# A recurrence's affine step, bonus and gate moved to features on the partitions, and GpSimd's arithmetic moved to VectorE, in a four-layer network

## The chip, the cores and the metric

The kernel runs on one core of one Trainium2 chip. The metric is the device time of one execution in microseconds, given as the median of several runs. The change touches the first two of four layers.

## What is computed

256 tokens of width 1024 pass two layers of a first block and two layers of a second one. The change lies in the first block, whose layer mixes three branches: attention over selected keys, a short convolution, and a recurrence with heads of 64. After the recurrence come, per token and head, a normalisation, an affine step, a bonus and a gate, and then the gated sum of the branches:

```python
    mean = jnp.mean(y, axis=-1, keepdims=True)
    var = jnp.mean(jnp.square(y - mean), axis=-1, keepdims=True)
    yn = ((y - mean) * lax.rsqrt(var + RW_GN_EPS) * ln_w.astype(f32).reshape(RW_HEADS, RW_HEAD_DIM)
          + ln_b.astype(f32).reshape(RW_HEADS, RW_HEAD_DIM))
    bonus = jnp.sum(r * kf * r_k.astype(f32), axis=-1, keepdims=True) * v
    out = (yn + bonus) * g.reshape(hs)
...
        up = jnp.einsum('bsgc,gcd->bsgd', branches, w_branch[l])
        gates = jax.nn.sigmoid(gate_pre + b_gate[l]).reshape(bsz, seq, N_BRANCH, D_MODEL)
        mixed = jnp.sum(gates * up, axis=2)
        h = h + mixed @ w_out[l]
```

## The kernel before, in words

Every weight matrix streams from HBM once. A panel lands in one of two `raw` buffers (SP queue); ACT makes its rounded high part `whi` (L184) and DVE the rest `wlo` (L185), three buffers each; PE multiplies in three terms: L206, L207 and L208, each 128x128 weights against 256 columns. These matmuls of the weights are most of PE's work. They write to PSUM pool `mm`, which has three banks (L125 names the pool); a bank comes free when ACT or DVE has read it.

A layer of the first block is `mix`. Three Python generators run in it as streams, `rwkv`, `attend` and `bulk`; each yields the cost that its author gave a step, times a factor of the table TUNE, and `interleave` always continues the stream that is behind. The order in which the streams emit, with a scheduler's reordering at build, is the order on each engine, and an engine takes its instructions strictly in that order.

- `rwkv`: `rw_prepare` (gate g at L784, bonus sums at L845), `rw_scores`, then `rw_solve` beside `rw_tokens`, then `rw_chain`. `rw_solve` inverts 32 small triangular matrices by 31 steps on DVE, one multiplication (L905) and one sum (L906) each, which grow to 512 columns; all read the buffer `lb`. After it come copies (L910), transposes (L917, L919), and 64 small matmuls twice (L926, L931). `rw_tokens` turns keys and values to tokens (L875, L879 on PE; copies L876, L880, L882 on ACT), and ends in `rw_rows`, which loads the affine rows by two DMAs and calls GpSimd four times per half (L1000 to L1003). `rw_chain` walks four chunks of 64 tokens (L946 to L979), and after every second one calls `rw_finish` (normalisation, with the affine step at L1019 and L1020).
- `attend`: queries flipped (L393, L672), key duplicates `kd` (L675), `kT` (L679), scores (L445), masking (L451), exponentials (L454), probabilities flipped and applied (L486, L488, L496, L498).
- `bulk`: gates of branch 1 into the four halves of two `gate` buffers (called `m`), each a matmul of 48 (`feature_pair`), two tanh on ACT (L1028) and, in `branch`, a product on DVE (L1035); the gates `th` of branch 2, again two buffers; branch 0; and at the end branch 2. Branches 0 and 2 are added into `m` by L1038 on DVE and L1039 on GpSimd.

Big temporary tiles come from one pool, `sl`, by `slot`: 21 buffers that are handed out in turn, so that a new tile takes the buffer of the tile that was given up longest ago, and its first writer waits for that tile's last reader:

```python
        v = (self.sx if extra else self.sl).tile([128, 1024], dt, tag="s4", name=name)[:, :n]
```

The tiles `m`, `th`, `lb`, `vt`, `lnwb`, `lng`, `gt`, `qT` and the split operands `op` all come from it.

Of the kernel before, what the change touches and what calls it, by code (L numbers as in the profile page):

```python
# [9 lines left out]
F32 = mybir.dt.float32  # L10
F32R = mybir.dt.float32r
I32 = mybir.dt.int32
AF = mybir.ActivationFunctionType
ALU = mybir.AluOpType
# [3 lines left out]
S = 256  # L18
# [482 lines left out]
class Block1:  # L501
# [6 lines left out]

    def rope_tables(self):
# [38 lines left out]
    def vectors(self, l):  # L548
# [6 lines left out]
                   ("k_a", one(w["rw_k_a"][l]), 4), ("r_k", w["rw_r_k"][l].rearrange("(a b) d -> a (b d)", b=2), 4)],  # L555
# [10 lines left out]
        vec = k.sp.tile([128, 204], F32, tag="vec", name="vec", bufs=2)  # L566
# [17 lines left out]
        out["ffn"] = vec[:, 70:202]  # L584
# [168 lines left out]
    def rw_prepare(self, l):  # L753
# [27 lines left out]
        self.gt = k.slot(2, 512, name="gtok")  # L781
        for t in range(2):
            ps = k.bank(k.rk, 512)
            nc.tensor.matmul(ps, lhsT=lo[:, 1, 128 * t:128 * t + 128], rhs=gup, start=True, stop=True)  # L784
            nc.scalar.copy(self.gt[:, t], ps)
# [55 lines left out]
        self.bonus = k.sp.tile([128, 2, 8], F32, tag="bonus", name="bonus", bufs=1)  # L841
        ps = k.bank(k.rk, 2, 8)
        for t in range(2):
            for b in range(4):
                nc.tensor.matmul(ps[:, t], lhsT=kx[:, b, 128 * t:128 * t + 128], rhs=k.c["sel"][:, 8 * b:8 * b + 8], start=b == 0, stop=b == 3)  # L845
        nc.vector.tensor_copy(self.bonus, ps)
        self.ar, self.bk = ar, bk

# [18 lines left out]
    def rw_tokens(self):  # L867
# [3 lines left out]
        vt = k.slot(2, 512, name="vt")  # L871
        for c in range(4):
# [8 lines left out]
            if c % 2:  # L881
                nc.scalar.copy(vt[:, c // 2], ps.rearrange("p a b -> p (a b)"))  # L882
            yield 1.5
        self.bkt, self.uv, self.vt = bkt, uv, vt
        self.rw_rows()
# [50 lines left out]
    def rw_chain(self):  # L936
# [3 lines left out]
        for c in range(4):  # L940
# [39 lines left out]
            yield 8.0  # L980
            if c % 2:
                self.rw_finish(c // 2)
                yield 8.0
        yc = k.operand(2)
        for j in range(2):
            k.split(k.flip_pair([self.yc[:, 0], self.yc[:, 1]], j), *yc[j])
        self.yo = yc
        yield 3.0

    def rw_rows(self):  # L990

        k, nc = self.k, self.k.nc
        lw = k.slot(2, 512, name="lnwb")
        nc.scalar.dma_start(out=lw[:, 0], in_=self.w["rw_ln_w"][self.l].partition_broadcast(128))
        nc.scalar.dma_start(out=lw[:, 1], in_=self.w["rw_ln_b"][self.l].partition_broadcast(128))
        self.lg = k.slot(2, 512, name="lng")
        for t in range(2):
# [484 lines left out]
```

## Time and profile before

| | us |
|---|---|
| median of 3 runs (lowest, highest) | 1742.14 (1742.01, 1744.76) |
| the profiled execution | 1742.93 |
| its span in the trace | 1740.9 |
| PE busy / DVE busy / ACT busy / GpSimd busy | 1700.2 / 1250.7 / 957.2 / 72.4 |

The profiled execution lies 0.8 us over the median, and 2.0 us of it lie outside the span. Times in the trace count from the span's start. The first layer's mixing runs up to about 349 us; the second layer of the first block repeats it some 515 us later, in the same order. Instruction lines (L905) are those of the kernel before; where a line of the changed kernel is meant, the text says so.

### The profile page before, as it was taken

The numbers are of one execution on the slowest core, as the hardware profiler recorded it, in microseconds if no ns is written. First come the engines' busy times: TensorE is split into PE (matmuls) and PEld (weight loads), VectorE is DVE, ScalarE is ACT, GpSimd is POOL, SyncE is SP. The second block draws the span as 40 slices with busy tenths as digits, with TensorE's granted clock in tenths as the row PEclk, the third lists the DMA queues.
The fourth block names the chain that finished last, engine by engine and source line by source line (L and its number), as shares of the span: only waits on it lengthen the run. The fifth ranks groups of instructions, "written<-read, shape, count | busy, mean of one in ns | idle before, by whom it ended". The sixth has DMA issues, their size and how long they took to land.

```text
span 1740.9 us, 30007 instructions
## 1 busy us (share of the span) xinstructions
PE 1700.2 (98%) x12016; PEld 1539.7 (88%) x12016; DVE 1250.7 (72%) x2464; ACT 957.2 (55%) x1688; POOL 72.4 (4%) x81
## 2 busy tenths in 40 slices
PE   8999899999999999899999999999999999999998
PEld 8988789899989988799899987788899887888997
DVE  6699947789957689757789857576666675666666
ACT  6554633556646544633555556666564566665643
POOL 2000201101000000201000000000000000000000
PEclk9999989999999999899999999999999999999999
DMA  7534323565556444314555565344445554444454
GB/s 229 171 111 128 115 74 101 178 192 186 181 179 209 127 137 129 98 62 146 169 189 177 186 211 170 129 157 142 157 147 172 191 172 144 146 149 158 155 171 134
DMA packets 217371, 268.89 MB, mean 154 GB/s; under 512 B 6570, under 2 KB 170716, under 8 KB 217232
## 3 DMA queue, kind: packets, MB, share of 16 engines
q1 hardware_dynamic: 213520, 262.81, 46.7%
q10 hardware_dynamic: 2944, 3.94, 0.8%
q8 instruction: 94, 1.54, 0.4%
q14 instruction: 45, 0.37, 0.1%
q0 software_dynamic: 768, 0.23, 0.1%
HBM read 265.91 MB, written 1.05 MB: 153 GB/s over the span
## 4 chain that ended last, share of the span: by engine, by line
PE 81%; DVE 11%; DMA 4%; ACT 3%; issue 2%; POOL 0%; ACTq 0%; SPq 0%; POOLq 0%; DVEq 0%
PE ps L206 15%; PE ps L207 15%; PE ps L208 15%; PE ps L246 8%; PE ps L244 8%; PE ps L245 8%; DVE wlo L185 4%; PE ps L445 2%; PE ps L393 2%; DMA raw<-in_ffn_down_dram 1%; DMA raw<-in_w_in_dram 1%; ACT whi L184 1%; PE ps L486 1%; DVE pr L905 1%; PE ps L949 1%
## 5 line engine op out<-in xcount | busy, mean ns | idle before, releaser
L185 DVE TENSOR_TENSOR wlo<-raw,whi 128x1024 fp32r<-128x1024 f32 (+2 forms) x504 | 615.4, 1224 | 302.2 <-ACT whi L184 289.1
L184 ACT ACTIVATE whi<-raw 128x1024 fp32r<-128x1024 f32 (+2 forms) x504 | 525.6, 1046 | 555.9 <-PE ps L207 292.8
L206 PE MATMUL ps<-op,whi 128*128 128x256 f32 x2464 | 710.6, 288 | 0.1
L207 PE MATMUL ps<-op,whi 128*128 128x256 f32 x2464 | 703.3, 285 | 1.2 <-DVE op L199 1.0
L208 PE MATMUL ps<-op,wlo 128*128 128x256 f32 x2464 | 702.2, 285 | 1.3 <-DVE wlo L185 1.2
L206 PEld LDWEIGHTS ps<-op,whi 128*128 128x128 f32 x2464 | 474.8, 193 | 11.2 <-issue 8.5
L207 PEld LDWEIGHTS ps<-op,whi 128*128 128x128 f32 x2464 | 475.2, 193 | 6.6 <-issue 4.3
L208 PEld LDWEIGHTS ps<-op,wlo 128*128 128x128 f32 x2464 | 474.9, 193 | 3.8 <-DVE wlo L185 1.8
L244 PE MATMUL ps<-whi,op 128*128 128x512 f32 (+2 forms) x784 | 306.2, 391 | 0.8 <-ACT qtok L1200 0.8
L245 PE MATMUL ps<-wlo,op 128*128 128x512 f32 (+2 forms) x784 | 302.2, 386 | 2.5 <-DVE wlo L185 2.5
L246 PE MATMUL ps<-whi,op 128*128 128x512 f32 (+2 forms) x784 | 303.2, 387 | 1.3 <-DVE op L199 1.3
L246 PEld LDWEIGHTS ps<-whi,op 128*128 128x128 f32 x784 | 148.5, 189 | 30.0 <-DVE op L199 2.2
L245 PEld LDWEIGHTS ps<-wlo,op 128*128 128x128 f32 x784 | 148.8, 190 | 29.4 <-DVE wlo L185 3.8
L244 PEld LDWEIGHTS ps<-whi,op 128*128 128x128 f32 x784 | 148.6, 190 | 29.4 <-issue 2.0
L454 ACT ACTIVATE e<-e,m 128x128 f32<-128x128 f32 (+1 forms) x160 | 70.9, 446 | 16.2 <-DVE m L451 15.8
L451 DVE CUSTOM_DVE_ANT_0 e<-ps,consts 128x128 f32<-128x128 f32 (+1 forms) x128 | 39.1, 351 | 15.5 <-PE ps L445 13.2
L199 DVE TENSOR_TENSOR op<-xt,op 128x512 fp32r<-128x512 f32 x48 | 32.2, 687 | 19.0 <-ACT op L198 18.8
L445 PE MATMUL ps<-qT 64*128 64x256 f32 (+1 forms) x256 | 35.8, 351 | 1.0 <-DVE m L451 0.8
L488 ACT COPY pt<-ps 128x384 f32<-128x384 f32 x64 | 28.8, 480 | 12.9 <-PE ps L486 7.6
L709 DVE SCALAR_TENSOR_TENSOR glu<-ps,vec,glu 128x254 f32<-128x254 f32 x72 | 34.4, 478 | 1.4
L1039 POOL TENSOR_TENSOR gate<-gate,up 128x512 f32<-128x512 f32 x16 | 26.0, 1627 | 212.3 <-DVE up L1038 169.6
L708 DVE SCALAR_TENSOR_TENSOR glu<-ps,vec,glu 128x255 f32<-128x255 f32 x72 | 34.3, 476 | 0.2
(337 smaller groups left out, 1562.7 us busy)
## 6 DMA issues: line engine op xcount, KB each, us to landing
raw<-in_w_in_dram SPq DMA_DIRECT2D x130, 1024.0 KB, 5.2
raw<-in_ffn_up_dram SPq DMA_DIRECT2D x44, 1024.0 KB, 5.1
raw<-in_ffn_down_dram SPq DMA_DIRECT2D x20, 1024.0 KB, 5.1
raw<-in_w_out_dram SPq DMA_DIRECT2D x16, 1024.0 KB, 5.2
raw<-in_w_branch_dram SPq DMA_DIRECT2D x24, 512.0 KB, 3.4
raw<-in_w_proj_a_dram SPq DMA_DIRECT2D x8, 1024.0 KB, 5.2
raw<-in_w_proj_b_dram SPq DMA_DIRECT2D x8, 1024.0 KB, 5.2
raw<-in_w_in_dram SPq DMA_DIRECT2D x8, 768.0 KB, 4.4
```

The lines of the kernel that those rows point to most:

```text
L184: nc.scalar.activation(out=hi, in_=v, func=AF.Copy)
L185: nc.vector.tensor_tensor(out=lo, in0=v, in1=hi.bitcast(F32), op=ALU.subtract)
L206: self.nc.tensor.matmul(ps, lhsT=hi[:, k], rhs=xh, start=k == 0, stop=False)
L207: self.nc.tensor.matmul(ps, lhsT=hi[:, k], rhs=xl, start=False, stop=False)
L208: self.nc.tensor.matmul(ps, lhsT=lo[:, k], rhs=xh, start=False, stop=k == nk - 1)
L244: self.nc.tensor.matmul(ps[t][:, :n], lhsT=xh, rhs=hi, start=kk == first, stop=False)
L245: self.nc.tensor.matmul(ps[t][:, :n], lhsT=xh, rhs=lo, start=False, stop=False)
L246: self.nc.tensor.matmul(ps[t][:, :n], lhsT=xl, rhs=hi, start=False, stop=kk == last)
L393: self.nc.tensor.transpose(ps[:, a, 128 * t:128 * t + 128], src[t][:, 128 * k:128 * k + 128], self.ident)
L445: nc.tensor.matmul(ps[b][:, a:a + n], lhsT=qt[r, 128 * t:128 * t + 128], rhs=kt[r, 0:n], start=True, stop=True)
L451: nc.vector.tensor_tensor_reduce(out=e[:, a:a + n], in0=ps[b][:, a:a + n], in1=mask[:, a:a + n], scale=1.0, scalar=3e38, op0=ALU.add, op1= ...
L454: nc.scalar.activation(out=e[:, a:a + n], in_=e[:, a:a + n], func=AF.Exp, scale=-1.0, bias=m[:, t:t + 1], accum_out=z[:, 2 * b + t:2 * b + ...
```

## The change

- The gate g is computed with features on the partitions (four 128x256 matmuls, not two of 128x512); ACT also writes `gl`, g times the affine weight, in four scaled copies. The affine weight and bias come as eight more rows of the small vectors that `vectors` loads and turns, by two short DMAs more.
- The bonus sums over a head (eight matmuls with 8 columns, L845, and a copy, L846) go. `rw_bonus`, called after the chain's first chunk, multiplies by a constant `same` (ones on two 64x64 diagonal blocks) in four 128x256 matmuls, which also spreads the sum; DVE multiplies by v (two operations from PSUM), adds the bias and multiplies by g (four).
- `rw_rows` goes, with its two DMAs and eight GpSimd operations, and so do the copies `vt` (L882) and L1019, L1020. At the end of the chain DVE multiplies the flipped result by `gl` and adds g times the rest, and then the result is split.
- `branch` adds with DVE (L1041 of the changed kernel).
- With `vt`, `lnwb` and `lng` gone and `gl` new, the pool `sl` hands out two tiles fewer per layer, in another order.

```diff
@@ -505,6 +505,11 @@
         self.sd = [k.cp.tile([128, 4, 128], F32, name=f"sd{i}") for i in range(2)]
         for s in self.sd:
             k.nc.gpsimd.memset(s, 0.0)
+
+        self.same = k.cp.tile([128, 128], F32, name="same")
+        k.nc.gpsimd.memset(self.same, 0.0)
+        for i in range(2):
+            k.nc.gpsimd.memset(self.same[64 * i:64 * i + 64, 64 * i:64 * i + 64], 1.0)
 
     def rope_tables(self):
 
@@ -552,7 +557,8 @@
         two = lambda v: v.rearrange("j (r p) -> (j r) p", p=128)
         groups = [[("b_gate", one(w["b_gate"][l]), 24), ("sc", two(w["sc_conv"][l]), 12), ("mu", one(w["rw_mu"][l]), 14),
                    ("w0", one(w["rw_w0"][l]), 4), ("a0", one(w["rw_a0"][l]), 4), ("k_k", one(w["rw_k_k"][l]), 4),
-                   ("k_a", one(w["rw_k_a"][l]), 4), ("r_k", w["rw_r_k"][l].rearrange("(a b) d -> a (b d)", b=2), 4)],
+                   ("k_a", one(w["rw_k_a"][l]), 4), ("r_k", w["rw_r_k"][l].rearrange("(a b) d -> a (b d)", b=2), 4),
+                   ("ln_w", one(w["rw_ln_w"][l]), 4), ("ln_b", one(w["rw_ln_b"][l]), 4)],
                   [("ffn0", two(w["ffn_conv"][l])[0:66], 66)], [("ffn1", two(w["ffn_conv"][l])[66:132], 66)]]
         out, loads = {}, []
         for g in groups:
...
@@ -778,11 +784,14 @@
             yield 3.0
         for dst, _, _ in two:
             nc.vector.tensor_scalar(out=flat(dst), in0=flat(dst), scalar1=0.5, scalar2=0.5, op0=ALU.mult, op1=ALU.add)
-        self.gt = k.slot(2, 512, name="gtok")
-        for t in range(2):
-            ps = k.bank(k.rk, 512)
-            nc.tensor.matmul(ps, lhsT=lo[:, 1, 128 * t:128 * t + 128], rhs=gup, start=True, stop=True)
-            nc.scalar.copy(self.gt[:, t], ps)
+        self.gt, self.gl = k.slot(4, S, name="g"), k.slot(4, S, name="gl")
+        for j in range(2):
+            ps = k.bank(k.rk, 2, S)
+            for i in range(2):
+                b = 2 * j + i
+                nc.tensor.matmul(ps[:, i], lhsT=gup[:, 128 * b:128 * b + 128], rhs=lo[:, 1], start=True, stop=True)
+                nc.scalar.activation(out=self.gl[:, b], in_=ps[:, i], func=AF.Copy, scale=v["ln_w"][:, b:b + 1])
+            nc.scalar.copy(self.gt[:, 2 * j:2 * j + 2], ps)
 
         ms = k.slot(16, 64, name="ms")
         nc.gpsimd.memset(ms, 1.0)
@@ -838,13 +847,21 @@
             for b in (2 * j, 2 * j + 1):
                 nc.vector.scalar_tensor_tensor(out=kx[:, b], in0=r[:, b], scalar=v["r_k"][:, b:b + 1], in1=a[:, b], op0=ALU.mult, op1=ALU.mult)
             yield 7.0
-        self.bonus = k.sp.tile([128, 2, 8], F32, tag="bonus", name="bonus", bufs=1)
-        ps = k.bank(k.rk, 2, 8)
-        for t in range(2):
-            for b in range(4):
-                nc.tensor.matmul(ps[:, t], lhsT=kx[:, b, 128 * t:128 * t + 128], rhs=k.c["sel"][:, 8 * b:8 * b + 8], start=b == 0, stop=b == 3)
-        nc.vector.tensor_copy(self.bonus, ps)
         self.ar, self.bk = ar, bk
+
+    def rw_bonus(self):
+
+        k, nc, v = self.k, self.k.nc, self.v
+        for j in range(2):
+            ps = k.bank(k.rk, 2, S)
+            for i in range(2):
+                nc.tensor.matmul(ps[:, i], lhsT=self.same, rhs=self.kx[:, 2 * j + i], start=True, stop=True)
+            u = k.temp(2, S, name="bv")
+            nc.vector.tensor_tensor(out=u, in0=self.vp[:, 2 * j:2 * j + 2, 64:], in1=ps, op=ALU.mult)
+            for i in range(2):
+                b = 2 * j + i
+                nc.vector.scalar_tensor_tensor(out=self.gt[:, b], in0=u[:, i], scalar=v["ln_b"][:, b:b + 1], in1=self.gt[:, b],
+                                               op0=ALU.add, op1=ALU.mult)
 
     def rw_scores(self):
 
@@ -868,7 +885,6 @@
 
         k, nc, bk = self.k, self.k.nc, self.bk
         bkt, uv = [k.slot(2, 512, name="bkt") for _ in range(2)], [k.slot(2, 512, name="uv") for _ in range(2)]
-        vt = k.slot(2, 512, name="vt")
         for c in range(4):
             ps = k.bank(k.rk, 4, 128)
             for b in range(4):
@@ -878,11 +894,8 @@
             for b in range(4):
                 nc.tensor.transpose(ps[:, b], self.vp[:, b, 64 * c:64 * c + 128], k.ident)
             nc.scalar.copy(uv[c // 2][64:128, c % 2], ps[64:128].rearrange("p a b -> p (a b)"))
-            if c % 2:
-                nc.scalar.copy(vt[:, c // 2], ps.rearrange("p a b -> p (a b)"))
             yield 1.5
-        self.bkt, self.uv, self.vt = bkt, uv, vt
-        self.rw_rows()
+        self.bkt, self.uv = bkt, uv
 
     def rw_solve(self):
 
@@ -978,29 +991,20 @@
                 self.yc = k.slot(2, 512, name="yc")
             nc.scalar.copy(self.yc[o, c // 2].rearrange("p (h d) -> p h d", d=64), y[o])
             yield 8.0
+            if c == 0:
+                self.rw_bonus()
+                yield 2.0
             if c % 2:
                 self.rw_finish(c // 2)
                 yield 8.0
         yc = k.operand(2)
         for j in range(2):
-            k.split(k.flip_pair([self.yc[:, 0], self.yc[:, 1]], j), *yc[j])
+            u, q = k.temp(2, S, name="yn"), slice(2 * j, 2 * j + 2)
+            nc.vector.tensor_tensor(out=u, in0=k.flip_pair([self.yc[:, 0], self.yc[:, 1]], j), in1=self.gl[:, q], op=ALU.mult)
+            nc.vector.tensor_tensor(out=u, in0=u, in1=self.gt[:, q], op=ALU.add)
+            k.split(u, *yc[j])
         self.yo = yc
         yield 3.0
-
-    def rw_rows(self):
-
-        k, nc = self.k, self.k.nc
-        lw = k.slot(2, 512, name="lnwb")
-        nc.scalar.dma_start(out=lw[:, 0], in_=self.w["rw_ln_w"][self.l].partition_broadcast(128))
-        nc.scalar.dma_start(out=lw[:, 1], in_=self.w["rw_ln_b"][self.l].partition_broadcast(128))
-        self.lg = k.slot(2, 512, name="lng")
-        for t in range(2):
-            v, g = self.vt[:, t], self.gt[:, t]
-            v3 = v.rearrange("p (h d) -> p h d", d=64)
-            nc.gpsimd.tensor_tensor(out=v3, in0=v3, in1=self.bonus[:, t].unsqueeze(2).to_broadcast([128, 8, 64]), op=ALU.mult)
-            nc.gpsimd.tensor_tensor(out=self.lg[:, t], in0=g, in1=lw[:, 0], op=ALU.mult)
-            nc.gpsimd.tensor_tensor(out=v, in0=v, in1=lw[:, 1], op=ALU.add)
-            nc.gpsimd.tensor_tensor(out=v, in0=v, in1=g, op=ALU.mult)
 
     def rw_finish(self, t):
         k, nc = self.k, self.k.nc
@@ -1016,8 +1020,6 @@
         nc.vector.tensor_reduce(out=m[:, 8:16], in_=sq, axis=AX.X, op=ALU.add)
         k.rstd(m[:, 8:16], 64, 64e-5)
         nc.vector.tensor_tensor(out=o3, in0=o3, in1=b8(m[:, 8:16]), op=ALU.mult)
-        nc.vector.tensor_tensor(out=o, in0=o, in1=self.lg[:, t], op=ALU.mult)
-        nc.vector.tensor_tensor(out=o, in0=o, in1=self.vt[:, t], op=ALU.add)
 
 
     def gate(self, l, g, j, th):
@@ -1036,7 +1038,7 @@
         else:
             u = k.temp(2, S, name="up")
             nc.vector.scalar_tensor_tensor(out=u, in0=th, scalar=1.0, in1=ps, op0=ALU.add, op1=ALU.mult)
-            nc.gpsimd.tensor_tensor(out=m, in0=m, in1=u, op=ALU.add)
+            nc.vector.tensor_tensor(out=m, in0=m, in1=u, op=ALU.add)
         return th
 
     def rwkv(self, l):
```

**The order, first place: ACT in the first layer, from a `whi` copy ahead of the first gate tanh after the solve has begun.** `gate_1528` and `gate_1541` are the second buffer of `m` before and now; `whi` are weight copies, `bkt` and `uv` those of `rw_tokens`, L923 of the changed kernel is L910. Before:

```order
L184 ACTIVATE whi_2119<-raw_2113 128x1024 [waits PE_49,Activation_49]
L1028 ACTIVATE gate_1528<-ps_1854,der_370 128x256 [waits PE_49]
L1028 ACTIVATE gate_1528<-ps_1854,der_370 128x256
L184 ACTIVATE whi_2332<-raw_2330 128x1024 [waits DMAHW3_49,DVE_49,PE_49]
L184 ACTIVATE whi_2371<-raw_2369 128x1024 [waits DMAHW4_49,DVE_49,PE_49]
L184 ACTIVATE whi_2375<-raw_2369 128x1024 [waits DVE_49,PE_49]
L1028 ACTIVATE gate_1528<-ps_2112,der_370 128x256 [waits PE_49]
L1028 ACTIVATE gate_1528<-ps_2112,der_370 128x256
```

Now:

```order
L184 ACTIVATE whi_2319<-raw_2317 128x1024 [waits DVE_49,DMAHW3_49,PE_49,Activation_49]
L184 ACTIVATE whi_2358<-raw_2356 128x1024 [waits DMAHW4_49,DVE_49,PE_49]
L184 ACTIVATE whi_2362<-raw_2356 128x1024 [waits DVE_49,PE_49]
L1030 ACTIVATE gate_1541<-ps_1854,der_376 128x256 [waits DVE_49]
L1030 ACTIVATE gate_1541<-ps_1854,der_376 128x256
L1030 ACTIVATE gate_1541<-ps_2099,der_376 128x256 [waits PE_49]
L1030 ACTIVATE gate_1541<-ps_2099,der_376 128x256
L923 COPY pr_1778<-tt_1777 64x16x32 [waits DVE_49]
```

The tanh into the second buffer of `m` stood behind a wait for PE; now it stands behind three weight copies and a wait for DVE. That wait is for the last multiplication of the solve, `pr_1778<-tt_1777,lb_1776 128x512`, because `gate_1541` has the buffer of `lb_1776`; before it had that of an older tile, long read. In the second layer `gate_6980` stands to `lb_7215` in the same way.

**Second place: PE at the same point.** `ps_1854` and `ps_2099` above are banks of the pool `mm`, whose third is `ps_2047`; `ps_2316` (before: `ps_2329`) is the next to be written there. Before:

```order
L207 MATMUL ps_2112<-op_262,whi_2119 128x256
L208 MATMUL ps_2112<-op_262,wlo_2120 128x256
L206 MATMUL ps_2329<-op_851,whi_2332 128x256 [waits Activation_49]
L207 MATMUL ps_2329<-op_851,whi_2332 128x256
L208 MATMUL ps_2329<-op_851,wlo_2333 128x256 [waits DVE_49]
```

Now:

```order
L208 MATMUL ps_2099<-op_268,wlo_2107 128x256
L206 MATMUL ps_2316<-op_857,whi_2319 128x256 [waits Activation_49]
L207 MATMUL ps_2316<-op_857,whi_2319 128x256
L208 MATMUL ps_2316<-op_857,wlo_2320 128x256 [waits DVE_49]
...
L206 MATMUL ps_2316<-op_858,whi_2319 128x256
L891 MATMUL ps_1936<-ident_82,bk_1324 128x128 [waits PE_49,Activation_49]
L891 MATMUL ps_1936<-ident_82,bk_1324 128x128
L891 MATMUL ps_1936<-ident_82,bk_1325 128x128 x2
L207 MATMUL ps_2316<-op_858,whi_2319 128x256
```

The instruction that takes a bank waits for ACT in both, before for L1028 on `ps_1854` at the head of the first list above, now for the same tanh in its new place. Queued behind it on PE now are the key and value transposes (L891, L895: L875, L879 before), and further on the flip of `kd`, the scores and the matmuls after the solve.

**Third place: DVE over the solve's last steps.** L918 and L919 of the changed kernel are L905 and L906; L930 and L932 are L917 and L919; L681 is L675. Before, at the step of 288 columns:

```order
L905 TENSOR_TENSOR pr_1776<-tt_1775,lb_1774 128x288 [waits DVE_49]
L906 TENSOR_REDUCE tt_1775<-pr_1776 128x12 [waits DVE_49]
L451 ISA e_1981,m_1982<-ps_1974,mask_1931 128x128 [waits PE_49]
L451 ISA m_1982 128x1
L451 ISA e_1981,m_1982<-ps_1974,mask_1931 128x256
L451 ISA m_1982 128x1
L451 ISA e_1987,m_1988<-ps_1975,mask_1931 128x128 [waits PE_49]
L451 ISA m_1988 128x1
L451 ISA e_1987,m_1988<-ps_1975,mask_1931 128x256
```

Now, from the step of 465 columns to the solve's end and on:

```order
L918 TENSOR_TENSOR pr_1778<-tt_1777,lb_1776 128x465 [waits DVE_49]
L919 TENSOR_REDUCE tt_1777<-pr_1778 128x15 [waits DVE_49]
L918 TENSOR_TENSOR pr_1778<-tt_1777,lb_1776 128x512 [waits DVE_49]
L919 TENSOR_REDUCE tt_1777<-pr_1778 128x16 [waits DVE_49]
L1037 SCALAR_TENSOR_TENSOR gate_1541<-gate_1541,ps_2047 128x512 [waits Activation_49]
L930 STREAM_TRANSPOSE ti_2162<-pr_1778 32x32x32 [waits Activation_49]
L930 STREAM_TRANSPOSE ti_2162<-pr_1778 32x32x32
L681 COPY kd_1961<-qk_184 128x256 [waits PE_49]
L681 COPY kd_1961<-qk_185 128x256
L932 STREAM_TRANSPOSE t1_2166<-pr_1778 32x1024 [waits DVE_49]
```

Before, the masking of attention (L451), `kd` and `kT`, the product L1035 and weight residues stood between the solve's steps. Now the last ten steps follow one another, and those operations stand behind the solve.

## Rows read from the trace of the kernel before

**Rows 1.** The page: busy time, share of the span, instructions; the chain by engine.
```profile
PE 1700.2 (98%) x12016; PEld 1539.7 (88%) x12016; DVE 1250.7 (72%) x2464; ACT 957.2 (55%) x1688; POOL 72.4 (4%) x81
...
PE 81%; DVE 11%; DMA 4%; ACT 3%; issue 2%; POOL 0%; ACTq 0%; SPq 0%; POOLq 0%; DVEq 0%
```

**Rows 2.** Windows: us; PE, PEld, DVE, ACT, POOL busy (count), PEclk, DMA, GB/s; layer 1.
```profile
168.15:180.00 11.85, 11.85 (x100) 11.69 (x100) 10.99 (x35) 4.51 (x7) 0.00 (x0) 1.00 0.58 178
180.00:215.00 35.00, 30.00 (x214) 25.28 (x213) 33.60 (x75) 24.88 (x65) 10.03 (x7) 0.95 0.35 106
215.00:243.00 28.00, 28.00 (x296) 25.18 (x295) 9.20 (x14) 9.52 (x20) 0.00 (x0) 0.76 0.07 20
243.00:342.00 99.00, 96.36 (x726) 87.21 (x724) 69.76 (x101) 44.60 (x68) 12.51 (x8) 1.00 0.44 144
```

**Rows 3.** Windows, the same stretches of layer 2.
```profile
695.50:729.00 33.50, 28.24 (x210) 23.76 (x210) 33.08 (x74) 24.77 (x65) 10.13 (x7) 1.00 0.36 111
729.00:758.00 29.00, 29.00 (x297) 26.30 (x298) 9.25 (x14) 9.29 (x20) 0.00 (x0) 0.71 0.06 19
```

**Rows 4.** Timeline of ACT: start us, us, what; gate tanh, both layer 1.
```profile
167.34 0.82 ACT L1028 ACTIVATE gate<-ps,der 128x256 f32<-128x256 f32 x2
...
233.89 1.54 ACT L1028 ACTIVATE gate<-ps,der 128x256 f32<-128x256 f32 x4
```

**Rows 5.** Timeline of PE: the query flips, ahead of 72 matmuls of weights.
```profile
167.11 1.04 PE L393 MATMUL ps<-ident,qk 128*128 128x128 f32 x8
```

**Rows 6.** Windows, a stretch in which PE has nothing but weights.
```profile
400.00:460.00 60.00, 60.00 (x503) 60.00 (x501) 54.28 (x84) 35.35 (x53) 1.08 (x2) 1.00 0.56 178
```

**Rows 7.** Timeline of DVE: the solve's first and last steps.
```profile
162.84 0.15 DVE L905 TENSOR_TENSOR pr<-tt,lb 128x2 f32<-128x2 f32 x1
...
206.10 0.68 DVE L906 TENSOR_REDUCE tt<-pr 128x16 f32<-128x512 f32 x1
```

**Rows 8.** Lines of DVE from 162.5 to 207: busy us, mean ns, idle before.
```profile
L905 DVE TENSOR_TENSOR pr<-tt,lb 128x2 f32<-128x2 f32 (+30 forms) x31 | 13.5, 436 | 0.6
L185 DVE TENSOR_TENSOR wlo<-raw,whi 128x1024 fp32r<-128x1024 f32 x9 | 11.8, 1311 | 0.0
...
L451 DVE CUSTOM_DVE_ANT_0 e<-ps,mask 128x128 f32<-128x128 f32 (+1 forms) x14 | 4.4, 348 | 1.0 <-PE ps L445 1.0
L1035 DVE SCALAR_TENSOR_TENSOR gate<-gate,ps 128x512 f32<-128x512 f32 x2 | 1.4, 678 | 0.0
```

**Rows 9.** Timeline of GpSimd and DVE while GpSimd runs, and just after.
```profile
193.76 3.78 POOL L1003 TENSOR_TENSOR vt<-vt,gtok 128x512 f32<-128x512 f32 x2
...
189.99 1.41 DVE L905 TENSOR_TENSOR pr<-tt,lb 128x300 f32<-128x300 f32 x1
...
192.81 2.08 DVE L185 TENSOR_TENSOR wlo<-raw,whi 128x1024 fp32r<-128x1024 f32 x1
...
198.51 0.57 DVE L905 TENSOR_TENSOR pr<-tt,lb 128x392 f32<-128x392 f32 x1
...
204.09 1.21 DVE L185 TENSOR_TENSOR wlo<-raw,whi 128x1024 fp32r<-128x1024 f32 x1
```

**Rows 10.** Chain that ended last, 160 to 245: one step, at two clocks.
```profile
226.93 1.90 PE ps L955 x16
...
237.26 1.07 PE ps L955 x16
```

**Rows 11.** Lines by form, 243 to 345 (DVE), 100 to 350 (PE), 226 to 243 (PE).
```profile
L1038 DVE SCALAR_TENSOR_TENSOR up<-th,ps 128x512 f32<-128x512 f32 x4 | 2.7, 683 | 1.7 <-PE ps L208 1.7
...
L1083 DVE TENSOR_SCALAR gate<-gate 128x512 f32<-128x512 f32 x4 | 1.7, 420 | 2.4 <-POOL gate L1039 2.4
...
L644 PE MATMUL ps<-kz,qiT 128*128 128x256 f32 x8 | 2.3, 392 | 0.0
L845 PE MATMUL ps<-consts,k 128*128 128x8 f32 x16 | 2.1, 247 | 0.7 <-DVE k L839 0.7
```

**Rows 12.** One line's answer: count, duration in ns (least, median, most).
```profile
L839 DVE SCALAR_TENSOR_TENSOR k<-r,vec,a x4: 475/476/478, 113.0 to 127.4; 128x256 f32<-128x256 f32 x4
```

More of the change, by code (lines that the diff above doesn't have):

```diff
@@ L565, in vectors @@
         yield
-        vec = k.sp.tile([128, 204], F32, tag="vec", name="vec", bufs=2)
+        vec = k.sp.tile([128, 210], F32, tag="vec", name="vec", bufs=2)
         c0 = 0
@@ L583, in vectors @@
             c0 += n
-        out["ffn"] = vec[:, 70:202]
+        out["ffn"] = vec[:, 78:210]
         self.next_v = out
```

## The prediction, made before the changed kernel ran

> **What bounds the kernel now.** The page comes first: PE is busy 98% of the span and holds 81% of the chain that ended last, DVE 72%, GpSimd 4% [rows 1]. A change that gives DVE or GpSimd less to do is worth only what PE stops waiting for, and one that makes PE wait costs that wait in full. So I looked for PE's losses where the change acts, in the mixing of the first layer, by windows [rows 2]. There are two kinds. Idle: between 180 and 215 us PE is busy 30.0 of 35, between 243 and 342 it is busy 96.4 of 99. And a granted clock below 1.00: 0.95 in the one stretch and 0.76 between 215 and 243, where PE is busy throughout, but at its lower level (1.2 GHz, not 2.4) for part of the time: one step of the chain took 1.90 us there and 1.07 us at the higher level [rows 10]. Ahead of the low clock PE had gaps and small matmuls, and few weights came (DMA share 0.07). Taking the clock's shortfall times the length of the stretch, the losses are 5.0 + 2.6 + 1.75 + 6.7 = 16.1 us per layer. The second layer has 5.3 and 8.4 in the two middle stretches [rows 3], much the same. Whatever the change does is to be set against these 16.
>
> The 6.7 have a cause that the change touches. The tanh of the gates `th` ran only at 233.89, four in a row [rows 4], because their buffers were those of `qT`, still read by the scores; until then the three banks of `mm` were full, and PE had few matmuls of weights to put between the small ones of the recurrence.
>
> **What the change moves.** The largest part is not in the code that it edits. The pool `sl` hands out two tiles fewer, and `m`'s second buffer becomes that of `lb`. Before, the tanh on `ps_1854` ran at 167.34 [rows 4]. Now it waits for the last multiplication of the solve (first place of the order), and PE's next bank waits for it (second place). Everything behind that PE instruction waits too, transposes, scores and all; behind the tanh on ACT stand the copy L910, the token copies and the next `whi`. Its price:
>
> PE's stop: in both orders 72 matmuls of weights stand between the query flips, which end at 168.15 [rows 5], and that instruction. Dense, one takes 60.0/503 = 0.119 us [rows 6], so PE would be through at 176.7; I add 1 us for a residue `wlo` that comes a step later, 177.6 rounded.
>
> The tanh's release: the solve began at 162.84, and its last multiplication ended when the last sum began, at 206.10 [rows 7], 43.3 us. Of that the change takes out: twelve of the masking operations at 0.348 with 1.0 us of waiting for PE ahead of them, 5.2; two L1035, 1.4; the copies for `kd` and `kT`, three that I put at 1.2, an estimate from L1035's 0.68; two residues of 1.31 (eight stood between the steps, six do now), 2.6 [rows 8]; and the slowing by GpSimd, 2.5: a step of 300 columns took 1.41 while GpSimd ran, where one of 392 just after took 0.57, so some 0.85 on each of three [rows 9]. Sum 12.9; 30.4 us are left, and the wait ends at 193.2. Two tanh at 0.41 [rows 4] make it 194.0. **PE stands from 177.6 to 194.0, 16.4 us**, and needs nothing in that time that is not queued behind the wait.
>
> What is late next: after it, transposes, scores and masking, which used to run beside the solve, share PE, ACT and DVE with L926, L931 and the chain. Small waits there: before, the idle of 180 to 215 was 5.0; I take 4, between 2 and 6. The clock: PE comes out of a long stop. Nothing in the trace shows a stop this long, so I bound its price by the low-clock losses of the two neighbouring stretches, 1.75 below and both together, 8.5, above, and take 5, nearer to the mixed small work of 215 to 243. Now that `th` has other buffers, the weights are there to fill with, which speaks against the upper end.
>
> **The edits themselves.** Bonus: four 128x256 matmuls at 0.39 (L644 [rows 11]) come on PE, 1.6 us, and eight of L845 at 0.25, some 2.0, go from a stretch where DVE is nearly as busy as PE: between a gain of 2.0 and a loss of 1.6, I take 0. Gate: ACT's four scaled copies lie in `rw_prepare` beside DVE work, ACT being busy 55% [rows 1]; without that cover they cost 4 x 0.41 = 1.6. Two short DMAs on GpSimd's queue and three memsets stand at the start or far ahead of their use: nothing; up to 1 us once if late. DVE gets two products from PSUM (0.68 each by L1038 [rows 11]), four operations at 0.48 [rows 12], four at the end of the chain (0.68) and eight adds (0.68), less four of L1019 and L1020 at 0.68 and a copy: 1.4 + 1.9 + 2.7 + 5.4 - 2.9 = 8.5 us per layer. In the tail DVE is busy 69.8 of 99 [rows 2], so it has room. There GpSimd's adds end with L1083 waiting 2.4 us in all [rows 11]; an add on DVE takes a third of the slowest ones. Against it stand two more DVE operations ahead of the last split. Of the 2.6 idle in the tail I leave 1.5.
>
> **The sum.** Per layer now: stop 16.4, late residue 1.0, waits 4, clock 5, tail 1.5, together 27.9, against 16.1: 11.8 more. Two layers: 23.6. From the profiled execution (1742.93) that is 1766.5; from the median, 0.8 lower, **1766**.
>
> **A rule weighed.** The rows first: while GpSimd ran 10.0 us in the solve [rows 2], DVE lost about 2.5 to 3.7 (a residue took 2.08 beside 1.21, too) [rows 9]. The Trainium skill (SBUF — State Buffer, "SBUF: two separate sides") says that GpSimd and VectorE share one port pair, held exclusively for a whole instruction, so that the other fully blocks. That speaks for the change: by it, the whole 10.0 would come back in the solve. In rows' terms, the solve would end 7.5 us earlier, the stop be 8.9, and the time 2 x 4.3 over the median, 1751. The rows show DVE going on beside GpSimd for most of that time, so I take 2.5; the other is a rival below.
>
> **The rivals.**
> (a) Faster. The stop does not come about or is short, because the solve's end or the tanh comes much earlier than I reckon. Then `th` is free, the weights fill the recurrence's small matmuls, GpSimd no longer slows the solve: waits 4 + clock 2 + tail 1.5 = 7.5 against 16.1, 8.6 less per layer, **1725**. It decides from a stop shorter than 16.4 - 11.8 = 4.6 us. Against it stands the queue: the wait is on the solve's last multiplication, and its 31 multiplications alone took 13.5 us, and each is followed by a sum that the next one needs [rows 8]. Chance 0.06.
> (b) No change: the stop comes, but the filled recurrence afterwards makes up for all of it, 1742 to 1746. It needs clock and waits near nothing, and the stop under 10. Chance 0.04.
> (c) DVE sets the pace: no stop, but the 8.5 us more of DVE per layer come onto the path, 1742 + 17 = **1759**. Against it: DVE's room in the tail. Chance 0.05.
> (d) GpSimd's share of the solve by the rule above: **1751**. Chance 0.10.
> (e) Worse: low clock and broken attention after the stop cost the upper bounds, 8.5 and 6, and the bonus its 1.6; 16.4 + 1.5 + 6 + 8.5 + 2 + 1.6 = 36 against 16.1, 20 more per layer, **1782**. Chance 0.12.
>
> **How the numbers follow.** The forecast has the rest, 0.63. Its own bounds: waits from 2 to 6, clock from 1.75 to 8.5, the stop within 2 either way. The range takes in (c), (d) and (e) and leaves out (a) and most of (b): 1748 to 1787. Differences of 0.2%, some 3.5 us, are about what a measurement can tell. Faster by more: (a), 0.06. Same: (b), 0.04. Slower: all else, 0.90.
>
> **What would show it.** On ACT, the second pair of branch 1's tanh at about 193 to 194, not 167; on PE one gap of some 16 us up to about 194 in the first layer, and its twin some 515 to 530 us later, waiting for ACT; on DVE the last thirteen pairs of steps with nothing between them but residues, and the solve's end near 193; the `th` tanh no longer four in a row; masking after the solve; no GpSimd row but memsets and DMA issues. Wrong would be the account if PE's stop were under 5 us or ended by something other than that tanh, if a new gap stood in the tail, or if DVE's adds appeared as what PE waits for.

## The result, and the profile after

| | before | changed |
|---|---|---|
| median, us (4 runs each) | 1743.45 | 1765.68 |
| lowest and highest | 1742.01 to 1748.08 | 1762.97 to 1766.75 |
| span of the profiled execution | 1740.9 | 1761.2 |

The ratio is 1.0123, with an interval of 1.0111 to 1.0136: the changed kernel is slower by 21 us. The page of the changed kernel has busy time first (section 1), then two lines of the costliest groups, each with the idle time before it:

```profile
PE 1691.8 (96%) x12008; PEld 1533.3 (87%) x12008; DVE 1250.2 (71%) x2490; ACT 957.6 (54%) x1692; POOL 26.0 (1%) x56
...
L185 DVE TENSOR_TENSOR wlo<-raw,whi 128x1024 fp32r<-128x1024 f32 (+2 forms) x504 | 606.9, 1207 | 327.1 <-ACT whi L184 308.5
...
L206 PE MATMUL ps<-op,whi 128*128 128x256 f32 x2464 | 711.1, 289 | 35.2 <-ACT gate L1030 34.3
```

Against [rows 1], PE is busy 8 us less in a span 20 us longer, and DVE as long as before. One line of PE has 35 us of idle time ahead of it, and 34.3 of these end with the gate tanh (L1030 of the changed kernel, L1028 before). PE's waits in the two mixings say that these are two stops:

```profile
PE ps L206 <- ACT gate L1030: 17.7, 1, 17.7
...
PE ps L206 <- ACT gate L1030: 16.5, 1, 16.5
```

The timelines of ACT, DVE and PE show the first of them, with DVE's last multiplication of the solve (L918 of the changed kernel) in between:

```profile
177.15 2.00 ACT L184 ACTIVATE whi<-raw 128x1024 fp32r<-128x1024 f32 x2 [5.69 <-DMA raw<-in_w_in_dram]
193.24 1.57 ACT L1030 ACTIVATE gate<-ps,der 128x256 f32<-128x256 f32 x4 [14.09 <-DVE pr L918]
...
192.52 0.69 DVE L918 TENSOR_TENSOR pr<-tt,lb 128x512 f32<-128x512 f32 x1
...
176.13 0.28 PE L208 MATMUL ps<-op,wlo 128*128 128x256 f32 x1
194.13 0.58 PE L206 MATMUL ps<-op,whi 128*128 128x256 f32 x1 [17.72 <-ACT gate L1030]
```

ACT has nothing to do for 14 us, since its next instruction is the tanh. The multiplication ends at 193.2, the tanh follows, and then PE. Before, the same tanh ran at 167.34 [rows 4]. The windows of layer 1 answer to [rows 2] (us; PE, PEld, DVE, ACT, POOL busy, granted clock, DMA share, GB/s):

```profile
168.15:180.00 11.85, 8.26 (x67) 7.88 (x66) 10.50 (x27) 5.07 (x5) 0.00 (x0) 1.00 0.56 179
180.00:215.00 35.00, 19.62 (x195) 17.56 (x196) 24.96 (x51) 13.73 (x36) 0.00 (x0) 0.61 0.10 31
215.00:243.00 28.00, 28.00 (x232) 24.19 (x232) 13.90 (x34) 17.68 (x47) 0.00 (x0) 0.94 0.25 76
243.00:354.00 111.00, 109.55 (x854) 100.37 (x852) 74.57 (x125) 49.89 (x75) 0.00 (x0) 1.00 0.42 134
```

PE lost 3.6 and 15.4 us to idle time in the first two stretches; the third has a granted clock of 0.94, not 0.76, but the second one of 0.61, not 0.95, so the low clock came earlier; and the last has 1.5 us idle, not 2.6 in a stretch 12 us shorter. Where the added time sits is told by one operation that closes each mixing and each feed-forward part, four matmuls of L357:

```profile
L357 PE MATMUL ps<-diag,ones x4: 273/275/275, 348.7 to 349.0; 128*128 128x128 f32 x4
L357 PE MATMUL ps<-diag,ones x4: 270/274/275, 534.9 to 535.2; 128*128 128x128 f32 x4
L357 PE MATMUL ps<-diag,ones x4: 273/275/275, 863.8 to 864.1; 128*128 128x128 f32 x4
```

```profile
L357 PE MATMUL ps<-diag,ones x4: 273/275/275, 358.9 to 359.2; 128*128 128x128 f32 x4
L357 PE MATMUL ps<-diag,ones x4: 270/274/275, 545.0 to 545.4; 128*128 128x128 f32 x4
L357 PE MATMUL ps<-diag,ones x4: 273/275/275, 884.1 to 884.4; 128*128 128x128 f32 x4
```

The first fence is the kernel before, the second the changed one. The first mixing ends 10.2 us later (358.9 against 348.7), the second 20.3 us later; the feed-forward part between them (to 545.0, 534.9 before) adds nothing, and neither does everything after, since the span is 20.3 us longer too.

### The profile page after: what moved, and what is told of

It reads as the page before. It is cut to its first block, busy times and chain, and to the rows that moved or that the text cites. A ratio compares the mean times of both kernels' runs of the same rounds, so it can differ in the third digit from the quotient of the medians.

```text
span 1761.2 us, 29954 instructions
## 1 busy us (share of the span) xinstructions
PE 1691.8 (96%) x12008; PEld 1533.3 (87%) x12008; DVE 1250.2 (71%) x2490; ACT 957.6 (54%) x1692; POOL 26.0 (1%) x56
## 4 chain that ended last, share of the span: by engine, by line
PE 80%; DVE 12%; DMA 4%; ACT 3%; issue 1%; ACTq 0%; SPq 0%; DVEq 0%
PE ps L206 14%; PE ps L208 14%; PE ps L207 14%; PE ps L244 8%; PE ps L245 8%; PE ps L246 8%; DVE wlo L185 3%; PE ps L445 2%; PE ps L393 2%; DMA raw<-in_w_in_dram 1%; PE ps L486 1%; DMA raw<-in_w_out_dram 1%; ACT whi L184 1%; DVE pr L918 1%; PE ps L496 1%
## 5 line engine op out<-in xcount | busy, mean ns | idle before, releaser
L185 DVE TENSOR_TENSOR wlo<-raw,whi 128x1024 fp32r<-128x1024 f32 (+2 forms) x504 | 606.9, 1207 | 327.1 <-ACT whi L184 308.5
L206 PE MATMUL ps<-op,whi 128*128 128x256 f32 x2464 | 711.1, 289 | 35.2 <-ACT gate L1030 34.3
L451 DVE CUSTOM_DVE_ANT_0 e<-ps,consts 128x128 f32<-128x128 f32 (+1 forms) x128 | 39.1, 351 | 16.9 <-PE ps L445 14.6
L199 DVE TENSOR_TENSOR op<-xt,op 128x512 fp32r<-128x512 f32 x48 | 32.2, 687 | 19.1 <-ACT op L198 19.1
L714 DVE SCALAR_TENSOR_TENSOR glu<-ps,vec,glu 128x255 f32<-128x255 f32 x72 | 34.3, 477 | 0.6 <-ACT glu L713 0.4
L713 ACT ACTIVATE glu<-ps,vec 128x256 f32<-128x256 f32 x72 | 33.0, 458 | 1.3 <-DVE glu L715 1.3
```

The lines of the kernel that those rows point to most:

```text
L185: nc.vector.tensor_tensor(out=lo, in0=v, in1=hi.bitcast(F32), op=ALU.subtract)
L206: self.nc.tensor.matmul(ps, lhsT=hi[:, k], rhs=xh, start=k == 0, stop=False)
L451: nc.vector.tensor_tensor_reduce(out=e[:, a:a + n], in0=ps[b][:, a:a + n], in1=mask[:, a:a + n], scale=1.0, scalar=3e38, op0=ALU.add, op1= ...
```

## The experiments

The theory: the time is lost where PE's bank waits for a tanh whose buffer is held until the solve ends, and this follows from how many buffers of the pool `sl` are held at that time, not from the edits as such. The main rival: the edits cost, that is the bonus matmuls, the DVE operations, or the sums on DVE.

**One buffer fewer in the kernel before.**

```diff
-        self.sl = pool("sl", 21)
+        self.sl = pool("sl", 20)
```

> The kernel before with one buffer fewer in the pool sl (20, not 21), and nothing else. By its order of instructions the second buffer of m is then that of lb, as in the change. Theory (the stop of PE behind that tanh is the cost): the branch-1 tanh at about 193 to 196 us, one gap of PE of 14 to 18 us in each of the two layers that ends with it, and a time of 1758 to 1768 us. Rival (the edits themselves cost, that is the bonus matmuls, the DVE operations, the added adds): no edit is in it, so 1740 to 1746 us and no such gap.

Measured: 1770.64 against 1744.31 on the same chip, ratio 1.0153 (1.0126 to 1.018). The timelines of ACT and PE:

```profile
195.65 1.57 ACT L1028 ACTIVATE gate<-ps,der 128x256 f32<-128x256 f32 x4 [15.87 <-DVE pr L905]
...
196.54 0.58 PE L206 MATMUL ps<-op,whi 128*128 128x256 f32 x1 [17.74 <-ACT gate L1028]
```

and PE's line from its page, for both layers:

```profile
L206 PE MATMUL ps<-op,whi 128*128 128x256 f32 x2464 | 713.2, 289 | 36.3 <-ACT gate L1028 35.5 <-ACT whi L184 0.7
```

Without a single edit of the change, the stop is there in its length and in its two places. The time lies 3 us over what I expected of it. Where these come from is not shown; in the profiled execution the clock between 215 and 243 was granted at 0.74, where the change has 0.94.

**The change with `gl` after the solve.**

```diff
-        self.gt, self.gl = k.slot(4, S, name="g"), k.slot(4, S, name="gl")
+        self.gt = k.slot(4, S, name="g")
...
-                nc.scalar.activation(out=self.gl[:, b], in_=ps[:, i], func=AF.Copy, scale=v["ln_w"][:, b:b + 1])
...
     def rw_bonus(self):
...
+        self.gl = k.slot(4, S, name="gl")
+        for b in range(4):
+            nc.scalar.activation(out=self.gl[:, b], in_=self.gt[:, b], func=AF.Copy, scale=v["ln_w"][:, b:b + 1])
```

> The change, but gl (g times the affine weight) is allocated and computed in rw_bonus, after the solve, so that it holds no buffer of sl through the solve. Theory: the tanh into m's second buffer waits for PE alone and runs near 167 us, no gap of PE over 3 us between 168 and 200, and a time of 1736 to 1746 us. Rival (the edits cost): all of them are still there, so 1760 us or more.

Measured: 1736.76 against 1744.31, ratio 0.9962 (0.9948 to 0.9976). A line of ACT's timeline, and PE's line from the page:

```profile
167.50 0.84 ACT L1032 ACTIVATE gate<-ps,der 128x256 f32<-128x256 f32 x2 [1.76 <-PE ps L208]
```

```profile
L206 PE MATMUL ps<-op,whi 128*128 128x256 f32 x2464 | 710.2, 288 | 0.6 <-ACT whi L184 0.6
```

The tanh is back at 167.5 and PE's stop is gone. All the arithmetic of the change is still there, and the kernel is faster than the one before. So `gl`, held from `rw_prepare` through the solve, is what took the buffer.

**The change with two tiles fewer near the solve, `gl` early.**

```diff
-        xs = k.slot(32, 32, name="xs")
+        xs = t1
...
-        kd = k.slot(2, 256, name="kd")
+        kd = k.temp(2, 256, name="kd")
```

> The change as it is, gl early, but with two tiles fewer asked of sl near the solve: xs lies in the unused rows of t1, and kd comes from the small temporaries. By its order the tanh into m's second buffer waits for PE (the query flips), not for the solve. Theory: no stop of PE over 4 us between 168 and 200, 1732 to 1745 us. Rival (gl's early place or the edits cost by themselves): 1755 us or more.

Measured: 1738.27 against 1742.51, ratio 0.9972 (0.9962 to 0.9982). The tanh on ACT, and PE's line:

```profile
173.09 0.84 ACT L1030 ACTIVATE gate<-ps,der 128x256 f32<-128x256 f32 x2
```

```profile
L206 PE MATMUL ps<-op,whi 128*128 128x256 f32 x2464 | 712.4, 289 | 0.8 <-ACT whi L184 0.8
```

The tanh runs at 173 and PE's stop is gone. A second, independent way of relieving the pool takes the loss away too, with `gl` where the change has it. The edits are not the cost.

**The sums alone, both ways.** In the kernel before, the line of `branch` alone is moved to DVE; in the change it is moved back.

```diff
-            nc.gpsimd.tensor_tensor(out=m, in0=m, in1=u, op=ALU.add)
+            nc.vector.tensor_tensor(out=m, in0=m, in1=u, op=ALU.add)
```

> The kernel before with the branch sums alone moved from GpSimd to DVE. Theory: the tail of each layer's mixing loses waits for GpSimd, 0 to 1.5 us per layer, so 1738 to 1743 us. Rival (DVE is the bound in the tail and the adds lengthen it): 8 adds at 0.68 on the path, 5 us per layer, 1752 us.

Measured: 1735.14 against 1744.31, ratio 0.9952 (0.9937 to 0.9967), some 8 us less and beyond what I expected. The line of the residues on DVE in the tail, 243 to 345, first of the kernel before, then with the sums on DVE; and the tail's window:

```profile
L185 DVE TENSOR_TENSOR wlo<-raw,whi 128x1024 fp32r<-128x1024 f32 x27 | 37.1, 1377 | 11.3 <-ACT whi L184 11.2
```

```profile
L185 DVE TENSOR_TENSOR wlo<-raw,whi 128x1024 fp32r<-128x1024 f32 x29 | 35.5, 1224 | 11.9 <-ACT whi L184 11.9
```

```profile
243.00:342.00 99.00, 98.72 (x756) 90.72 (x755) 71.87 (x120) 47.01 (x70) 0.00 (x0) 1.00 0.44 144
```

A residue takes 1.22 us on average where it took 1.38 (four of the 27 took 2.17 to 2.35, as the last section shows, and the others 1.21 to 1.23), PE's idle time falls from 2.6 [rows 2] to 0.3, and PE gets 756 matmuls done there, not 726. The first mixing ends at 344.7, 4.0 us earlier. DVE is not the bound in the tail.

> The change with the branch sums left on GpSimd. Theory: the stop behind the tanh stays, so 1764 to 1770 us, at most 3 us over the change. Rival (the adds on DVE are the cost): back to 1742 to 1750 us.

Measured: 1766.08 against 1744.31, ratio 1.0131 (1.0111 to 1.0151), the stop as in the change. The sums explain nothing of the loss; but beside the stop they also gain next to nothing, some 1.4 us by the ratios, which the two intervals do not tell from zero.

**Without GpSimd beside the solve.** The loop of `rw_rows` is left out and `self.lg = lw` put in its place, so the bonus, the gate and the affine products are missing from the result.

```diff
-        for t in range(2):
-            v, g = self.vt[:, t], self.gt[:, t]
...
-            nc.gpsimd.tensor_tensor(out=v, in0=v, in1=g, op=ALU.mult)
+        self.lg = lw
```

> The kernel before without the eight GpSimd operations of rw_rows per layer (L1000 to L1003: bonus times v, gate times affine rows); the loaded rows and the plain copies of v are read in their place. Theory (GpSimd slowed DVE in the solve by 2.5 to 3.7 us): in the stretch of the solve's steps from 300 columns on, the steps take 0.47 to 0.69 each as their neighbours do, the solve's last multiplication ends 2 to 4 us earlier than at 205.9, and the time is 1734 to 1743 us. Rival (DVE is blocked for the whole 10 us that GpSimd runs): the solve ends 8 to 10 us earlier, 1722 to 1732 us.

Measured: 1733.84 against 1742.51, ratio 0.9948 (0.993 to 0.9966), 9 us or 4.5 per layer: at the edge of the theory's range, short of the rival's. The solve's last multiplication ended at 202.0, 3.9 us earlier than at 205.9; the theory had 2 to 4 there and the rival 8 to 10. The lines of DVE over the solve's steps of layer 1, of the kernel before and of this one:

```profile
L905 DVE TENSOR_TENSOR pr<-tt,lb 128x2 f32<-128x2 f32 (+30 forms) x31 | 13.5, 436 | 0.6
L185 DVE TENSOR_TENSOR wlo<-raw,whi 128x1024 fp32r<-128x1024 f32 x9 | 11.8, 1311 | 0.0
...
L661 DVE TENSOR_SCALAR mask<-isc 128x384 f32<-128x384 f32 x1 | 1.2, 1202 | 0.0
```

```profile
L905 DVE TENSOR_TENSOR pr<-tt,lb 128x2 f32<-128x2 f32 (+30 forms) x31 | 10.6, 343 | 0.6
...
L185 DVE TENSOR_TENSOR wlo<-raw,whi 128x1024 fp32r<-128x1024 f32 x8 | 9.7, 1214 | 0.0
```

The multiplications lose 2.9 us. The residues lose 0.9 in all, and one of them has it: 2.08 at 192.81 [rows 9], where the others took 1.22. The mask operation L661 took 1.2 us with GpSimd beside it; without it, 0.35 (one line's answer: count, least, median and most ns):

```profile
L661 DVE TENSOR_SCALAR mask<-isc x1: 352/352/352, 168.3 to 168.3; 128x384 f32<-128x384 f32 x1
```

Together GpSimd's operations slowed DVE by 2.9 + 0.9 + 0.8 = 4.6 us in layer 1, and half of the gain, 4.5, is close to that number. It is an average only: in the profiled execution, the longest of the four (1738.65), the first mixing ended 4.0 us earlier (344.7) and the second, with a clock of 0.53 from 725 to 754, only 3.8 in all (860.0). The steps ran from 162.8 to 205.2 before and from 164.7 to 201.3 here, 5.8 us less; the layer's other instructions between them moved a little as well.

**The sums on GpSimd, `gl` late.** The second experiment with the line of `branch` back on GpSimd.

> The change with gl computed after the solve, and with the branch sums left on GpSimd. Theory (the adds on DVE are worth the same with and without the other edits, 9 us, when no stop is there): 1743 to 1748 us, 7 to 10 over the run with gl late alone (1736.8). Rival (the adds are worth little beside the other edits, as the run of the change with its sums on GpSimd had it, 0.4 us): 1735 to 1739 us.

Measured: 1739.27 against 1742.51, ratio 0.9976 (0.9964 to 0.9989). Between both: by the ratios the sums on DVE are worth 2.4 us beside the other edits, and 8.4 alone; the intervals of the two runs behind the 2.4 overlap. The edits without the sums give 4.2. The gains of the parts overlap; through what was not settled.

**`gl` late and two tiles fewer.** Both edits above together.

> The change with gl late and with the two tiles fewer. Theory: the gates th get buffers at the end of the solve (their tanh before 215, not at 234 as in the kernel before), so that weights fill the recurrence's small matmuls: 1725 to 1736 us, below the run with gl late alone (1736.8). Rival (the low clock and the small matmuls of that stretch do not depend on it): 1735 to 1739 us.

Measured: 1739.01 against 1742.51, ratio 0.9975 (0.9964 to 0.9986), not below the run with `gl` late alone. By the order of its instructions the first buffer of `th` is that of a tile last read in `rw_prepare`, so nothing holds it; its tanh still ran at 232, and the clock was as low as before:

```profile
232.25 0.83 ACT L1032 ACTIVATE gate<-ps,der 128x256 f32<-128x256 f32 x2
```

```profile
215.00:243.00 28.00, 28.00 (x279) 24.82 (x276) 10.00 (x18) 9.14 (x19) 0.00 (x0) 0.76 0.06 20
```

By its order that tanh stands on ACT behind the copy of the chain's first result, which ran at 231.77. So the late `th` tanh comes with the order, not with the wait for `qT` alone.

**A version that beats both.** The kernel before with the sums on DVE and `rw_rows` called later.

```diff
         self.bkt, self.uv, self.vt = bkt, uv, vt
-        self.rw_rows()
...
             yield 8.0
+            if c == 0:
+                self.rw_rows()
+                yield 2.0
             if c % 2:
...
-            nc.gpsimd.tensor_tensor(out=m, in0=m, in1=u, op=ALU.add)
+            nc.vector.tensor_tensor(out=m, in0=m, in1=u, op=ALU.add)
```

> The kernel before with the branch sums on DVE, and with rw_rows (its two DMAs and eight GpSimd operations per layer) called after the chain's first chunk and not beside the solve. Theory (GpSimd beside the solve costs some 4 us per layer, apart from what the sums cost): no GpSimd arithmetic between the solve's first and last step, the solve's last multiplication 2 to 6 us earlier than in the kernel before, and 1724 to 1731 us. Rival (what the two edits give overlaps, as it did between the sums and the other edits of the change): 1732 to 1737 us, like the run with the sums alone (1735.1).

> The same without the move of the sums: the kernel before with rw_rows called after the chain's first chunk. Theory: 1732 to 1738 us, as the run without GpSimd beside the solve had it (1733.8). Rival (GpSimd's work costs the same wherever it lies, since DVE runs in the chain too): 1740 to 1745 us.

Measured: 1732.31 against 1742.71, ratio 0.9943 (0.9931 to 0.9956), the lowest median here, though its interval overlaps that of the sums alone, and just inside the rival's range; without the sums 1738.48, ratio 0.9975 (0.9965 to 0.9984), just over the theory's. So what the two edits give overlaps too, as the rival had it. The solve's last multiplication ended 1.9 us earlier than in the kernel before (204.0) where 2 to 6 was expected, and the expectation failed in one more point: two of GpSimd's operations per layer, those that need only `vt` and the bonus, still ran beside the solve, as the timeline of GpSimd in the first of the two shows.

```profile
168.29 1.12 POOL L1002 TENSOR_TENSOR vt<-vt,bonus 128x512 f32<-128x512 f32 x1 [5.33 <-PE ps L207]
186.42 1.14 POOL L1002 TENSOR_TENSOR vt<-vt,bonus 128x512 f32<-128x512 f32 x1 [17.01 <-ACT vt L882]
234.81 2.51 POOL L1003 TENSOR_TENSOR lng<-gtok,lnwb 128x512 f32<-128x512 f32 x2 [47.24 <-DMA lnwb<-in_rw_ln_w_dram]
```

So in these two kernels GpSimd still works beside the solve. In the runs of the change with `gl` late and with two tiles fewer all of its arithmetic is away, with the work kept, on DVE: GpSimd is busy 0.00 us there from 168 to 342, and the gain is 5 to 7 us.

## Why the prediction was right, point by point

**Direction and size: right, 1766 forecast, 1765.68 measured.** As a difference 24 us were forecast and 21 to 22 measured; a layer became 10.2 and 10.1 us longer, where 11.8 was reckoned. The mechanism is the one named: the tanh into `m`'s second buffer waits for the solve. It stands at 193.24 where 193 to 194 was forecast, PE stops from 176.4 to 194.1 (forecast 177.6 to 194.0), and the second layer has the twin. The runs with one buffer fewer, with `gl` late and with two tiles fewer show it from three sides.

**The terms were less good than their sum.**

- The stop: 16.4, and 1.0 for a late residue, forecast; 17.7 in layer 1 and 16.5 in layer 2 measured. Right; the residue was not late, PE ran dense to its stop.
- The solve: 30.4 us forecast from its first step to the tanh's release; 161.9 to 193.2, 31.3, measured. Of the 12.9 that I took off, GpSimd had 2.5; it was 4.6, since I had counted only three steps and neither the mask operation nor the slow residue. The rest, 10.4, was then too large by 3.0. That the tanh's release came at 193.2 to the tenth is luck: the solve also began 0.9 us earlier than I had it.
- Waits after the stop: 4 forecast (2 to 6). Measured 1.3 us in both layers: 21.0 less 19.6 between 194 and 215 in layer 1, 25.0 less 23.7 between 720 and 745 in layer 2. Too high; that attention and chain filled each other's waits is my reading, not shown.
- The clock: 5 forecast (1.75 to 8.5). After the stop it was granted at 0.66 for 21 us and 0.94 for 28 in layer 1, and at 0.79 for 25 in layer 2:

```profile
194.00:215.00 21.00, 19.62 (x195) 17.56 (x196) 11.79 (x27) 12.97 (x35) 0.00 (x0) 0.66 0.01 2
...
720.00:745.00 25.00, 23.73 (x242) 20.88 (x243) 13.12 (x33) 15.77 (x42) 0.00 (x0) 0.79 0.00 1
```

That is 7.1 + 1.7 = 8.8 and 5.3 us, with the reckoning of [rows 2]; just over the range in one layer, the value taken in the other. But it is not what I had priced. Right behind the stop, up to 205, the shortfall of layer 1 is some 2 us. The rest lies from 205 to 220, with the small matmuls that follow the solve and with scores, and the kernel before had the same there, only later. First the changed kernel, then the one before:

```profile
205.00:215.00 10.00, 10.00 (x111) 8.50 (x109) 2.67 (x18) 6.01 (x22) 0.00 (x0) 0.50 0.01 2
215.00:220.00 5.00, 5.00 (x35) 4.52 (x34) 0.35 (x1) 0.74 (x3) 0.00 (x0) 0.67 0.00 0
```

```profile
220.00:230.00 10.00, 10.00 (x103) 9.39 (x102) 2.59 (x3) 3.09 (x6) 0.00 (x0) 0.50 0.01 2
230.00:240.00 10.00, 10.00 (x89) 8.30 (x88) 2.90 (x5) 3.71 (x9) 0.00 (x0) 0.86 0.00 0
```

So the 6.7 of before did not go in layer 1; it moved up with the end of the solve. In layer 2 less of it is left, 3.4 us after 730, where the kernel before had 8.4.

- The tail: 1.5 forecast, 1.5 and, in layer 2, 2.5 measured.

The measured terms of layer 1, 17.7 + 1.3 + 8.8 + 1.5 = 29.3, less the 16.1 of before, make 13.2, and the layer became 10.2 longer: such a balance is good to some 3 us.

**What was wrong though the sum was right.** Rival (a), the time without the stop, was put at 1725; the two runs that have the change without the stop took 1736.8 and 1738.3, 5 to 7 us under the kernel before, not 17. The step that failed is the one that put the low clock between 215 and 243 down to the gates `th` waiting for `qT`'s buffer, and let it go with the wait. Rival (a) has 2 us left for the clock. The run with `gl` late has 8.6 in layer 1, 1.0 from 180 to 215 and the rest here:

```profile
215.00:243.00 28.00, 28.00 (x254) 24.31 (x252) 10.12 (x19) 9.83 (x21) 0.00 (x0) 0.73 0.07 20
```

With 3.0 us of idle time up to 215 and 1.2 in the tail that makes 12.8, against 16.1 before and 7.5 in (a), and its first mixing did end 3.1 us earlier (345.6). The run with both edits has, by its order, the first buffer of `th` free, and the same late tanh and the same 0.76. What the stop itself costs is then smaller than I had it: from 0.9962 to 1.0123 it is some 28 us for both layers, where my two prices, 1766 and 1725, have 41 between them. Seen so, two errors of 10 to 13 us cancelled: the time without the stop was put too low, and the price of the stop too high.

**The edits.** Two costs from rows of other lines were near. The bonus matmuls show as eight instructions of 0.379 in 1.9 us, 1.6 forecast, and the added DVE operations took 0.68 and 0.47 each, as forecast:

```profile
L1041 DVE TENSOR_TENSOR gate<-gate,up 128x512 f32<-128x512 f32 x8 | 5.5, 687 | 0.1
L863 DVE SCALAR_TENSOR_TENSOR g<-bv,vec,g 128x256 f32<-128x256 f32 x4 | 1.7, 474 | 0.0
```

They have next to no idle time ahead of them and DVE had room, so rival (c) did not come about. But what the sums on GpSimd had cost was mis-sized: I left 1.1 us per layer to be gained in the tail, and moving them alone gave 4.2. I had priced the waits of L1083 [rows 11] and not the slowing of four residues and of one split (L199, 1.77 where 0.69 is usual). Why this gain nearly vanishes beside the stop stays open; in the profiled executions the clock after the stop differed between the two runs (0.66 and 0.94 with the sums on DVE, 0.76 and 1.00 with them on GpSimd), in layer 1, which would hide some 2 to 4 us, but that one comparison does not show it to be the reason.

**The rule that was weighed.** Removing GpSimd's work from the solve gave back 4.6 us of DVE's time of the 10.0 that GpSimd was busy there. That lies between my 2.5 and the 10 that would follow if DVE had been blocked all the time. The Trainium skill (SBUF — State Buffer, "SBUF: two separate sides") limits the lock on DVE's side to operations that use both ports or have two SBUF inputs. The rows agree with this limit as far as they go; rival (d) had left it out. Slowed beside GpSimd were four of the two-input multiplications, by 0.4 to 1.0 us each, a two-input residue, by 0.9, and the mask operation, by 0.8; the mask operation has one input, and no row shows which ports it uses. Not slowed were the masking of attention (L451, one input from PSUM: 0.35 on average with and without GpSimd) and the solve's own sums (L906, one input). Rival (d), which took the whole 10.0, did not happen.

## What to carry to other kernels

Count the buffers that a pool holds at its tightest moment before and after a change: a tile that is made earlier and kept longer can cost more than all the arithmetic of the edit, and the instruction that then waits can belong to quite another part of the program. Look at what stands behind it on its engine and which PSUM bank it should free. And when two engines share work, price what the one does to the other's durations, operation by operation, and not only the waits that name it.

## What the runs showed of the hardware that was not expected

When an addition on GpSimd and a two-input operation on DVE meet, the one that began later takes longer, by nearly the rest of the other. Two such pairs of the kernel before, in the tail of layer 1:

```profile
265.06 1.28 POOL L1039 TENSOR_TENSOR gate<-gate,up 128x512 f32<-128x512 f32 x1 [67.52 <-DVE up L1038]
265.20 2.23 DVE L185 TENSOR_TENSOR wlo<-raw,whi 128x1024 fp32r<-128x1024 f32 x1 [0.21 <-ACT whi L184]
...
311.13 1.22 DVE L185 TENSOR_TENSOR wlo<-raw,whi 128x1024 fp32r<-128x1024 f32 x1
311.35 2.14 POOL L1039 TENSOR_TENSOR gate<-gate,up 128x512 f32<-128x512 f32 x1 [2.98 <-DVE up L1038]
```

In the first pair the residue came 0.14 us after the addition and took 2.23, where 1.22 is usual. In the second it came first and took 1.22, and the addition took 2.14, where 1.28 is usual. Of the 27 residues there only the four that began within 0.21 us after an addition were slow; the mean of 1.38 hides that. A one-input mask operation of 384 columns took 1.20 us when it began 0.14 after a GpSimd operation of 1.12 us, and 0.35 without it.

After PE's long stop the clock was first granted at the lower level for dense matmuls of weights too (1.2 GHz: 0.41 us each from 194.5 to 196.2, 0.28 before the stop and again at 197.9).
